# The eight relative-bias tables of a hybrid decoder layer: one product for all of them, and stores that read one partition repeatedly

## The chip, the core and the metric

The kernel runs on one core of a Trainium2 chip, in one launch. The metric is the device time of one execution in microseconds (us), from several runs of the same program on one chip.

## What is computed

The reference is one decoder layer on 1024 tokens of width 1024: a gated feed-forward layer, a mixer with two groups of heads (differential attention and a gated linear recurrence), and a second feed-forward layer, each behind a norm that is shifted and scaled by a conditioning vector. The change touches one input of the attention only, the relative bias:

```python
def t5_bucket(rel):
    n = jnp.maximum(rel, 0)
    ...
    return jnp.where(n < max_exact, n, large)

def diff_attention(q, k, v, rel_bias, lam):
    ...
        s = jnp.einsum('bmqd,bmkd->bmqk', qb, k, preferred_element_type=jnp.float32) * scale
        rel = (start + jnp.arange(Q_BLOCK, dtype=jnp.int32))[:, None] - kpos[None, :]
        bias = jnp.take(rel_bias, t5_bucket(rel), axis=0)
        s = s + jnp.transpose(bias, (2, 0, 1)).astype(jnp.float32)[None]
        s = jnp.where((rel >= 0)[None, None], s, -jnp.inf)
```

There are 32 buckets and 8 maps (4 heads with two each), so `rel_bias` is 32 x 8. A score's bias depends on the distance of query and key alone, and is constant from a distance of 128 on.

## The kernel before

All activations lie transposed or in token rows of 512 columns. Every large product is done in three passes on split fp32 operands (`mm3`, lines 63 to 66): a high part and a remainder, made by one ScalarE cast (line 57) and one VectorE subtraction (line 60). The first feed-forward layer (`f1`) multiplies in blocks: for each of eleven pairs of hidden columns p it runs units of twelve matmuls of 128x512. The last pair is p = 10, its units come in the order 1, 6, 2, 5, 7, 3, 4 with two halves m = 0 and 1 each. A unit of product 1 is followed by a ScalarE copy of its PSUM bank (`f1vp`, line 503), and the unit of product 6 with the same m then adds onto that same bank. The finished hidden parts (`f1vs`, `f1vu` and so on) are stored to DRAM (`f1g`, `f1gt`), combined in place by VectorE (line 391), stored again, and read back (`f1b`) for the second half of the layer, the down products (`f1ps`), which begin at 503.9 us.

The order of the work is not the order of the text. Each piece is recorded as an operation with an engine, an estimated duration, what it reads and writes, and a rank (a due time); `Plan.run` (line 220) then simulates the engines and emits, for each, the operation that can start first, the lower rank first. A tile has a tag with a fixed number of places; the next tile of that tag waits until all use of the last one has ended. The tag `acc` has one place. DMAs all go through SyncE (SP): its queue is in program order, an instruction that has to wait keeps back what stands behind it, and eight DMA semaphores are used in turn, so that a DMA also waits for the eighth before it.

Beside the last units of `f1`, between 450 and 492 us, the kernel builds the bias tables (`bias_table`, lines 991 to 1008). For each map m: VectorE copies the map's column of `rel_bias` to 128 columns (`rbb`, line 996); TensorE multiplies that with a one-hot matrix of buckets (`oh`, line 998), so that all 128 partitions of PSUM hold the same row of 256 biases; VectorE takes off the last bucket's value (lines 1003 and 1004) and appends 128 columns of -1e30 (line 1005); and SP stores the 128 equal rows of 384 elements to a DRAM buffer `wd{m}` (line 1008). The store makes the attention's later load (`near_bias`, line 1356) a plain strided read, one column further left for each query row. The tile `wt{m}` has the tag `acc`, and table m starts after table m - 1.

Then come the scalars of attention and recurrence (`lam_and_rnn_columns`, line 1049): four small loads of the lambda vectors into `lt` (line 1054, tag `acc` too, after the last table's store), a product and a sum on VectorE (lines 1012 and 1013), an exponential on ScalarE (line 1057), and a chain of some two dozen tiny VectorE instructions for a log-sigmoid (lines 1033 to 1047) with an exponential of its own (line 1060).

The names in the profile's rows: `psw` is the bias product, `wt` the table, `wd` the DRAM buffer, `f1w` a split weight, `f1B` a split activation, `kh` and `kl` the split keys of the attention, which SP copies from 64 partitions to the other 64 (line 1352).

Of the kernel before, what the change touches and what calls it, by code (L numbers as in the profile page):

```python
# [10 lines left out]
F32 = mybir.dt.float32  # L11
F32R = mybir.dt.float32r
AF = mybir.ActivationFunctionType
ALU = mybir.AluOpType
# [3 lines left out]
P = 128  # L18
# [7 lines left out]
HEADS = 4  # L26
QK = 64
NBK = 32
EPS = 1e-6
MASK = -1.0e30  # L30
# [14 lines left out]
def layer(tc, I, out):  # L45
    nc = tc.nc
    V, A, G, T = nc.vector, nc.scalar, nc.gpsimd, nc.tensor
    stack = ExitStack()

    def load(o, i):  # L50
        nc.sync.dma_start(out=o, in_=i)
# [27 lines left out]
    def bank(tag, nm):  # L79
        return psp[0].tile([P, TG], F32, tag=tag, bufs=BANKS[tag], name=nm)  # L80
# [47 lines left out]
    wd = [dram.tile([P * 384], F32, name=f"wd{m}") for m in range(2 * HEADS)]  # L128
# [4 lines left out]
    class Plan:  # L133
# [52 lines left out]
        def op(self, eng, fn, dur, r=(), w=(), rank=0.0, lat=None, hold=(), after=(), port=None):  # L186
            durs = dict(zip(eng, dur)) if isinstance(eng, tuple) else {eng: dur}
            deps = {self.last[k] for k in (*r, *w, *after) if k in self.last}
            since = max((self.end.get(k, 0.0) for k in (*r, *w, *after) if k not in self.last), default=0.0)
            for k in w:  # L190
                deps.update(self.reads.get(k, ()))
            n = len(self.ops)
            for k in r:
                self.reads.setdefault(k, []).append(n)
            for k in w:
                self.last[k], self.reads[k] = n, []
            places = sorted({self.place(k) for k in (*r, *w, *hold)} - {None})
            for s in places:
                self.left[s] += 1
            if port is None:  # L200
                tags = {t for k in r if self.place(k) for t in self.tag[self.place(k)]}
                port = not tags & self.PSUM
            self.ops.append((durs, fn, rank, lat, sorted(deps), places, since, tuple(w), port,
                             isinstance(eng, tuple)))
# [120 lines left out]
    PE, ACT, DVE, POOL, SP = "PE", "Act", "DVE", "Pool", "SP"  # L325
# [10 lines left out]
    def new_tile(plan, key, tag, shape=None, dt=F32):  # L336
        def make(t=tag if isinstance(tag, str) else tag[0]):
            if t in BANKS:
                return bank(t, key)
            s = shape or [P, TG]  # L340
            if t in KEPT:
                return KEPT[t].tile(s, dt, tag=t, name=key)
            return phase["fp"].tile(s, dt, tag=t, bufs=FFN_PLACES[t], name=key)

        plan.tile(key, tag, make)
# [412 lines left out]
    plan = Plan(FFN_PLACES, None, 0.2)  # L758
    op, tile, the = plan.op, plan.tile, plan.get
# [141 lines left out]
    def due1(n, k=0):  # L901
        if n < 4 * EARLY:
            return 21.0 + 5.0 * (4 * (n // 6) + k) + T_MM3 * (n % 6)
        return 62.0 + 2.58 * (n - 4 * EARLY)
# [8 lines left out]
    for k in range(KC):  # L913
        at = due1(6 * (k // 4), k % 4) - 5
# [70 lines left out]
    for n, (b, hf) in enumerate(halves):  # L985
        u = 40 + 8 * n
        ada_half(f1, b, hf, due1(u), 2.8, f1.when(u - 2), lambda ps, b=b, hf=hf: ada_columns(b, hf, ps), 1.3,
                 w=[("mod", b, hf)])


    def bias_table(m, at):
        rbb, ps, wt, b31 = (f"{s}{m}" for s in ("rbb", "psw", "wt", "b31_"))
        new_tile(plan, wt, "acc")
        new_tile(plan, rbb, "k2")
        new_tile(plan, ps, ("tr", "av"))
        op(DVE, lambda: V.tensor_copy(the(rbb)[0:NBK, 0:P], the("rb")[0:NBK, m : m + 1].to_broadcast([NBK, P])), 0.2, r=["rb"],
           w=[rbb], rank=at, after=[f"wt{m - 1}"] if m else [("mod", 7, 1)])
        op(PE, lambda: T.matmul(the(ps)[:, 0:256], lhsT=the(rbb)[0:NBK, 0:P], rhs=the("oh")[0:NBK, 0:256], start=True, stop=True), 0.45,
           r=[rbb, "oh"], w=[ps], rank=at)

        def table():
            b = fp.tile([P, 1], F32, tag="b31", bufs=1, name=b31)
            V.tensor_copy(b, the(ps)[:, 0:1])
            V.tensor_scalar(the(wt)[:, 0:256], the(ps)[:, 0:256], b, None, ALU.subtract)
            V.memset(the(wt)[:, 256:384], MASK)

        op(DVE, table, 0.6, r=[ps], w=[wt], rank=at, hold=[rbb])
        op(SP, lambda: load(wd[m].rearrange("(q t) -> q t", t=384), the(wt)[:, 0:384]), 0.3, r=[wt], w=[f"wd{m}"], rank=at)

    def lam_sums():  # L1010
        pr = fp.tile([P, 2, QK], F32, tag="arow", bufs=1, name="lpr")
# [37 lines left out]
    def lam_and_rnn_columns(at):  # L1049
        new_tile(plan, "lt", "acc", [P, 4, QK])  # L1050
        tile("ldt", "z", lambda: small("ldt", 2))
        tile("lw", "z", lambda: small("lw", 16))
        for j, nm in enumerate(("lam_q1", "lam_k1", "lam_q2", "lam_k2")):
            op(SP, lambda j=j, nm=nm: load(the("lt")[:, j, :], I[nm].to_broadcast([P, QK])), 0.3, w=[("lt", j)],
               rank=at - 4, after=["wd7"])
        op(DVE, lam_sums, 0.5, r=[("lt", j) for j in range(4)], w=["ldt"], rank=at)
        op(ACT, lambda: A.activation(the("ldt"), the("ldt"), AF.Exp), 1.5, r=["ldt"], w=["ldt"], rank=at)
        op(DVE, lam_value, 0.2, r=["ldt", "smc"], w=["nlam"], rank=at)
        op(DVE, minus_abs, 0.15, r=["smc"], w=["lw"], rank=at, after=["wd7"])
        op(ACT, lambda: A.activation(the("lw")[:, 4:8], the("lw")[:, 0:4], AF.Exp), 0.2, r=["lw"], w=["lw"], rank=at)  # L1060
        op(DVE, log_sigmoid, 2.0, r=["lw", "smc"], w=["rcol"], rank=at)
# [2 lines left out]
    tile("rb", "z", lambda: small("rb", 8))  # L1064
    op(SP, lambda: load(the("oh")[0:NBK, 0:256], I["onehot"]), 0.1, w=["oh"], rank=due1(126), after=f1.when(126))
    op(SP, lambda: load(the("rb")[0:NBK], I["rel_bias"]), 0.1, w=["rb"], rank=due1(126), after=f1.when(126))
    for m in range(2 * HEADS):
        bias_table(m, due1(128 + 1.5 * m))
    lam_and_rnn_columns(due1(142))


# [72 lines left out]
    for j in range(2):  # L1144
        rc, hi, lo, ps = f"rc{j}", f"wch{j}", f"wcl{j}", f"pc{j}_0"
# [3 lines left out]
           rank=t2 - 10, after=[("f1d4_4", 0)])  # L1149
# [6 lines left out]
        for k in range(KC):  # L1156
# [3 lines left out]
               r=[hi, lo, *x], w=[ps], rank=t2 + j)  # L1160
        op(ACT, lambda j=j, ps=ps: A.activation(the("qf00")[:, j, :], the(ps), AF.Copy, scale=0.125 if j == 0 else 1.0),
           T_CAST, r=[ps], w=[("qf00", j)], rank=t2)
# [29 lines left out]
    for tag in ("tr", "av", "mm"):  # L1192
        bank(tag, tag)
    plan = Plan(
        {"mm": 2, "tr": 1, "z": 8, "av": 1, "d": 2, "p": PB, "qk": 6, "qf": 4, "xr": 2, "v": 4, "at": 2,
         "ln": 3, "nb": 1, "xh": 8, "h": 32, "wh": 4, "raw": 3}, was
    )
    op, tile, the = plan.op, plan.tile, plan.get
# [535 lines left out]
    for j in range(2):  # L1734
        n = next(nch)
        chunk(n)
        f = f"qf0_{j}_0"
# [41 lines left out]
    for dc in range(KC):  # L1779
        n = n0 + dc  # L1780
# [11 lines left out]
    for dc in range(6):  # L1792
        n = n0 + 8 + dc
# [5 lines left out]
    for n, k in enumerate(ORDER):  # L1799
        sq = "n3a" if n == 0 else f"n3s{k}"  # L1800
        if n:
            mkt(sq, "qf", [P, TG], bufs=4)
        op(ACT, lambda sq=sq, k=k: A.activation(the(sq), the(f"x21_{k}"), AF.Square), 0.5, r=[f"x21_{k}"], w=[sq],
           rank=FIRST + 130)
        if n:
            op(DVE, lambda sq=sq: V.tensor_tensor(the("n3a"), the("n3a"), the(sq), ALU.add), 0.62, r=["n3a", sq],
               w=["n3a"], rank=FIRST + 130)
# [24 lines left out]
    plan = f2.plan  # L1832
    op, tile, the = plan.op, plan.tile, plan.get
# [14 lines left out]
    def due2(n):  # L1848
        return t0 + 2.6 * n
# [18 lines left out]
    for k in (0, 4, 1, 5, 2, 6, 3, 7):  # L1868
        x, x2, o = x3[k], f"x21_{k}", 2 * KC + k
        op(DVE, lambda x=x, x2=x2, o=o: V.scalar_tensor_tensor(  # L1870
            the(x), the(x2), gmc[:, o : o + 1], the("n3r"), ALU.mult, ALU.mult), T_DVE, r=["n3r", x2], w=[x],
           rank=t0 - 10)
# [25 lines left out]
    for hf in range(2):  # L1898
# [3 lines left out]
           w=[row], rank=due2(u), after=f2.when(u - 6))  # L1902
        ada_half(f2, 8, hf, due2(u), 5.0, f2.when(u - 6), lambda ps, hf=hf: gate3(hf, ps), 1.2, [row], [row])
        op(SP, lambda hf=hf, row=row: load(g3d[:, hf * TG : (hf + 1) * TG], the(row)[0:1]), 0.1, r=[row],
           w=[f"g3d{hf}"], rank=due2(u + 18))
# [126 lines left out]
def build(shapes):  # L2032
    import concourse.bacc as _bacc
    import concourse.tile as _tile

    nc = _bacc.Bacc("TRN2", target_bir_lowering=False, num_devices=1)
    aps = {n: nc.dram_tensor(f"in_{n}", s, F32, kind="ExternalInput").ap() for n, s in shapes.items()}
    out = nc.dram_tensor("out_0", (1, S, D), F32, kind="ExternalOutput").ap()
    with _tile.TileContext(nc, schedule_with_timeline_sim=True) as tc:
        layer(tc, aps, out)  # L2040
    return nc
# [10 lines left out]
```

## Time and profile before

| | |
|---|---|
| three runs, median (lowest, highest) | 1808.46 us (1805.84, 1812.81) |
| the profiled execution, own time | 1807.46 us |
| its span, first to last instruction | 1805.7 us |
| TensorE (PE) busy | 1769.0 us, 98% of the span |
| VectorE (DVE) busy | 1426.6 us, 79% |
| ScalarE (ACT) busy | 855.2 us, 47% |
| DMA | 297.50 MB, all but 1.5 MB through SP's queue |
| mean granted TensorE clock | 0.992 |

The profile is of one execution. Its times are counted from the first instruction. A row names the line, the engine, the operation and its tiles as out<-in; busy time is the sum of the instructions' durations. Matmuls overlap in the engine's pipeline, so the step from one start to the next tells what a matmul costs, not its duration.

### The profile page before, as it was taken

The page shows a single profiled execution, that of the slowest core. Times are in us where ns is not written, and L with a number is a line of the kernel's source. Part 1 is how long each engine was busy: PE and PEld are TensorE (multiplying, and loading weights), DVE is VectorE, ACT ScalarE, POOL GpSimd, SP SyncE. Part 2 cuts the span into 40 slices and gives each one's busy share as a digit, 9 for nine tenths or more (in the row PEclk, how much of TensorE's full clock was granted, in tenths as well). Part 3 has the DMA queues.
Part 4 walks back from the last instruction along what each step waited for, and adds up shares of the span by engine and source line. Part 5 has one row for each costly group of instructions (what it writes and reads, how often), then busy time and mean ns, then how long its engine had stood idle before and what let it go on. Part 6 is the DMA issues. An engine that isn't in the chain of part 4 may idle for free.

```text
span 1805.7 us, 23739 instructions
## 1 busy us (share of the span) xinstructions
PE 1769.0 (98%) x8182; PEld 1462.4 (81%) x8182; DVE 1426.6 (79%) x2725; ACT 855.2 (47%) x1485; POOL 13.0 (1%) x28
## 2 busy tenths in 40 slices
PE   8999999999999999999999989999999999999997
PEld 7878888888788888788888778878888888888886
DVE  3799998998778779789787786598777666589798
ACT  3543334333454334676675854453333333364344
POOL 0000000000000001000000000000000000000000
PEclk7999999999999999999999999999999999999999
DMA  9635666554597672412112435314434323497862
GB/s 277 203 111 200 204 214 199 187 198 135 195 350 278 222 251 94 105 47 65 53 59 65 129 99 186 120 54 170 155 123 139 127 96 111 152 362 266 284 213 93
DMA packets 230137, 297.50 MB, mean 165 GB/s; under 512 B 16733, under 2 KB 125438, under 8 KB 230018
## 3 DMA queue, kind: packets, MB, share of 16 engines
q1 hardware_dynamic: 230018, 296.00, 49.7%
q8 instruction: 64, 1.05, 0.2%
q14 instruction: 55, 0.45, 0.1%
HBM read 228.30 MB, written 63.44 MB: 162 GB/s over the span
## 4 chain that ended last, share of the span: by engine, by line
PE 87%; DVE 9%; DMA 2%; ACT 1%; issue 1%; SPq 0%; DVEq 0%; ACTq 0%
PE f1b L64 7%; PE f1b L66 7%; PE f1b L65 7%; PE f2b L64 7%; PE f2b L65 7%; PE f2b L66 7%; PE pc L64 5%; PE pc L66 5%; PE pc L65 5%; PE f2ps L64 4%; PE f2ps L65 4%; PE f2ps L66 4%; PE f1ps L66 3%; PE f1ps L65 3%; PE f1ps L64 3%; PE psd L874 2%
## 5 line engine op out<-in xcount | busy, mean ns | idle before, releaser
L64 PE MATMUL f1b<-f1B,f1w 128*128 128x512 f32 x616 | 245.8, 399 | 0.8 <-ACT f1vs L512 0.8
L65 PE MATMUL f1b<-f1B,f1w 128*128 128x512 f32 x616 | 242.7, 394 | 3.6 <-DVE f1w L60 3.6
L66 PE MATMUL f1b<-f1B,f1w 128*128 128x512 f32 x616 | 242.9, 394 | 0.0
L64 PE MATMUL f2b<-f2B,f2w 128*128 128x512 f32 x440 | 171.6, 390 | 1.7 <-ACT f2vq L488 1.4
L65 PE MATMUL f2b<-f2B,f2w 128*128 128x512 f32 x440 | 171.3, 389 | 0.6 <-DVE f2w L60 0.6
L66 PE MATMUL f2b<-f2B,f2w 128*128 128x512 f32 x440 | 171.2, 389 | 0.0
L65 PEld LDWEIGHTS f1b<-f1B,f1w 128*128 128x128 f32 x616 | 116.3, 189 | 29.9 <-DVE f1w L60 4.8
L64 PEld LDWEIGHTS f1b<-f1B,f1w 128*128 128x128 f32 x616 | 116.2, 189 | 29.2 <-issue 2.9
L66 PEld LDWEIGHTS f1b<-f1B,f1w 128*128 128x128 f32 x616 | 116.2, 189 | 26.6
L60 DVE TENSOR_TENSOR f2w<-f2r,f2w 128x512 fp32r<-128x512 f32 x124 | 84.7, 688 | 66.3 <-ACT f2w L57 65.2
L64 PE MATMUL pc<-h,wch 128*128 128x512 f32 x320 | 129.0, 403 | 0.0
L57 ACT ACTIVATE f2w<-f2r 128x512 fp32r<-128x512 f32 x124 | 76.5, 628 | 105.8 <-issue 40.2
L65 PE MATMUL pc<-h,wcl 128*128 128x512 f32 x320 | 125.3, 391 | 0.0
L66 PE MATMUL pc<-h,wch 128*128 128x512 f32 x320 | 125.2, 391 | 0.0
L57 ACT ACTIVATE f1w<-f1r 128x512 fp32r<-128x512 f32 x124 | 76.8, 628 | 96.9 <-PE f1b L66 40.7
L66 PE MATMUL f1ps<-f1o,f1d 128*128 128x512 f32 x308 | 121.2, 394 | 0.0
L64 PE MATMUL f1ps<-f1o,f1d 128*128 128x512 f32 x308 | 121.2, 393 | 0.0
L65 PE MATMUL f1ps<-f1o,f1d 128*128 128x512 f32 x308 | 121.0, 393 | 0.0
L64 PE MATMUL f2ps<-f2d,f2o 128*128 128x512 f32 x308 | 119.9, 389 | 0.1
L66 PE MATMUL f2ps<-f2d,f2o 128*128 128x512 f32 x308 | 119.8, 389 | 0.0
L65 PE MATMUL f2ps<-f2d,f2o 128*128 128x512 f32 x308 | 119.8, 389 | 0.0
L64 PEld LDWEIGHTS f2b<-f2B,f2w 128*128 128x128 f32 x440 | 82.6, 188 | 20.0 <-ACT f2vq L488 1.8
(410 smaller groups left out, 3937.9 us busy)
## 6 DMA issues: line engine op xcount, KB each, us to landing
ar<-in_ada_w SPq DMA_DIRECT2D x112, 256.0 KB, 3.2
f2r<-in_ffn_w SPq DMA_DIRECT2D x44, 512.0 KB, 3.7
f1r<-in_ffn_w SPq DMA_DIRECT2D x40, 512.0 KB, 4.3
f1wa<-in_ffn_w SPq DMA_DIRECT2D x38, 512.0 KB, 5.0
f2wa<-in_ffn_w SPq DMA_DIRECT2D x38, 512.0 KB, 5.8
f1b<-f1gt SPq DMA_DIRECT2D x44, 256.0 KB, 5.8
f2b<-f2gt SPq DMA_DIRECT2D x44, 256.0 KB, 6.0
rc<-in_w_in SPq DMA_DIRECT2D x20, 512.0 KB, 3.7
```

The source lines that it names most:

```text
L57: A.activation(hi, src, AF.Copy)
L60: (eng or V).tensor_tensor(lo, src, hi.bitcast(F32), ALU.subtract)
L64: T.matmul(ps, lhsT=wh, rhs=xl, start=first, stop=False, skip_group_check=more)
L65: T.matmul(ps, lhsT=wl, rhs=xh, start=False, stop=False, skip_group_check=more)
L66: T.matmul(ps, lhsT=wh, rhs=xh, start=False, stop=last, skip_group_check=more)
L874: T.matmul(the(ps)[:, b : b + 1], lhsT=the(aw)[:, n, :], rhs=cact[:, 4 * h + n : 4 * h + n + 1], start=h == 0 and n == 0, stop=h == 1 and ...
```

## The change

One product makes all eight tables: the 32 x 8 matrix `rel_bias` itself is the left operand, so that map m's row of 256 biases lies on partition m alone. One copy, one subtraction and one fill on 8 partitions finish the tables. The eight stores stay, each of 128 rows of 384 elements to the same DRAM buffer, but each now reads its one partition m 128 times (a step of 0 in the source). Nothing that reads `wd` is changed. The tables are one tile `wt`, due at unit 136 in place of 128 to 138.5.

```diff
-    def bias_table(m, at):
-        rbb, ps, wt, b31 = (f"{s}{m}" for s in ("rbb", "psw", "wt", "b31_"))
-        new_tile(plan, wt, "acc")
-        new_tile(plan, rbb, "k2")
-        new_tile(plan, ps, ("tr", "av"))
-        op(DVE, lambda: V.tensor_copy(the(rbb)[0:NBK, 0:P], the("rb")[0:NBK, m : m + 1].to_broadcast([NBK, P])), 0.2, r=["rb"],
-           w=[rbb], rank=at, after=[f"wt{m - 1}"] if m else [("mod", 7, 1)])
-        op(PE, lambda: T.matmul(the(ps)[:, 0:256], lhsT=the(rbb)[0:NBK, 0:P], rhs=the("oh")[0:NBK, 0:256], start=True, stop=True), 0.45,
-           r=[rbb, "oh"], w=[ps], rank=at)
+    def bias_tables(at):
+        n = 2 * HEADS
+        new_tile(plan, "wt", "acc")
+        new_tile(plan, "psw", ("tr", "av"))
+        op(PE, lambda: T.matmul(the("psw")[0:n, 0:256], lhsT=the("rb")[0:NBK, 0:n], rhs=the("oh")[0:NBK, 0:256],
+                                start=True, stop=True), 0.45, r=["rb", "oh"], w=["psw"], rank=at, after=[("mod", 7, 1)])
 
         def table():
-            b = fp.tile([P, 1], F32, tag="b31", bufs=1, name=b31)
-            V.tensor_copy(b, the(ps)[:, 0:1])
-            V.tensor_scalar(the(wt)[:, 0:256], the(ps)[:, 0:256], b, None, ALU.subtract)
-            V.memset(the(wt)[:, 256:384], MASK)
-
-        op(DVE, table, 0.6, r=[ps], w=[wt], rank=at, hold=[rbb])
-        op(SP, lambda: load(wd[m].rearrange("(q t) -> q t", t=384), the(wt)[:, 0:384]), 0.3, r=[wt], w=[f"wd{m}"], rank=at)
+            b = fp.tile([P, 1], F32, tag="b31", bufs=1, name="b31")
+            V.tensor_copy(b[0:n], the("psw")[0:n, 0:1])
+            V.tensor_scalar(the("wt")[0:n, 0:256], the("psw")[0:n, 0:256], b[0:n], None, ALU.subtract)
+            V.memset(the("wt")[0:n, 256:384], MASK)
+
+        op(DVE, table, 0.6, r=["psw"], w=["wt"], rank=at)
+        for m in range(n):
+            op(SP, lambda m=m: load(wd[m].rearrange("(o q t) -> o q t", o=1, t=384),
+                                    the("wt")[m : m + 1, 0:384].unsqueeze(1).to_broadcast([1, P, 384])), 0.3, r=["wt"],
+               w=[f"wd{m}"], rank=at)
...
-    for m in range(2 * HEADS):
-        bias_table(m, due1(128 + 1.5 * m))
+    bias_tables(due1(136))
```

The planner emits another order from there on. On SP before, the first stores of tables stand between the stores of hidden parts (each row with what it waits for; `DMAHW` are the eight semaphores of the DMAs, used in turn):

```order
L51 DMA f1g_9_166<-f1vv_0_4004 128x512 [waits DMAHW3_49,DVE_49]
L51 DMA wd_119<-wt_4119 128x384 [waits DMAHW4_49,DVE_49]
L51 DMA f1g_9_144<-f1vs_4086 128x512 [waits DMAHW5_49,DVE_49]
L51 DMA wd_120<-wt_4147 128x384 [waits DMAHW6_49,DVE_49]
L51 DMA f1gt_9_188<-f1vs_4086 128x512 [waits DMAHW7_49,DVE_49]
```

and the lambda loads follow twenty-four rows after the first of these stores:

```order
L51 DMA lt<-in_lam_q 128x64 [waits DMAHW4_49,DMAHW5_49,DMAHW1_49,DMAHW0_49]
L51 DMA lt<-in_lam_k 128x64
L51 DMA lt<-in_lam_q 128x64
L51 DMA lt<-in_lam_k 128x64 [waits DMAHW7_49]
L51 DMA f1b_3_4464<-f1g_3_160 128x512 [waits DVE_49]
```

With the change, SP's queue at the same place (after six stores like the first two here):

```order
L51 DMA wd_125<-wt 128x1x384 [waits DMAHW2_49]
L51 DMA wd_126<-wt 128x1x384 [waits DMAHW3_49]
L51 DMA f1g_9_144<-f1vs_4086 128x512 [waits DMAHW4_49,DVE_49]
L51 DMA lt<-in_lam_q 128x64 [waits DMAHW5_49,DMAHW3_49,DMAHW6_49,DMAHW2_49,DMAHW7_49,DMAHW1_49,DMAHW0_49]
L51 DMA lt<-in_lam_k 128x64
L51 DMA lt<-in_lam_q 128x64
L51 DMA lt<-in_lam_k 128x64
L51 DMA f1g_9_177<-f1vu_0_3910 128x512 [waits DVE_49]
L51 DMA f1gt_9_188<-f1vs_4086 128x512 [waits DVE_49]
```

The eight stores now stand in a row, the store of the hidden part `f1vs` of p = 9 has moved behind them, and the lambda loads, which need the place of `wt`, stand right after it and wait for the stores.

On VectorE with the change, beside the last units of p = 9 and the first of p = 10 (`f1vu`, `f1vs`, `f1vp`: hidden parts of p = 9; `lw`: the log-sigmoid):

```order
L518 TENSOR_TENSOR f1vu_1_3947<-f1vu_1_3947,f1b_9_1_4041 128x512
L522 TENSOR_TENSOR f1vu_0_3910<-f1vu_0_3910,f1vu_1_3947 128x512
L391 TENSOR_TENSOR f1vs_4086<-f1vp_0_3866,f1vs_4086 128x512
L1034 TENSOR_SCALAR lw<-lw 128x4
L1035 RECIPROCAL lw<-lw 128x4
```

and, twenty-two tiny instructions on `lw` further (new line numbers are one above the old):

```order
L1046 TENSOR_SCALAR rcol<-lw 128x4
L1047 TENSOR_SCALAR rcol<-lw 128x4
L1048 TENSOR_SCALAR rcol<-smc 128x8
L1013 TENSOR_TENSOR lpr<-lt 128x128
L1014 TENSOR_REDUCE ldt<-lpr 128x2
L391 TENSOR_TENSOR f1vp_0_3866<-f1vu_0_3910,f1vp_0_3866 128x512
L60 TENSOR_TENSOR f1w_4176<-f1s_0_3976,f1w_4176 128x512
```

Before, VectorE had all of p = 9 and nearly all weights of p = 10 behind it when it came to `lw` and `lt`; now these two stand ahead of the last work of p = 9 and of the weights from product 5 on.

On ScalarE before, at the first units of p = 10:

```order
L503 ACTIVATE f1vp_0_4209<-f1b_10_0_4175 128x512
L57 ACTIVATE f1w_4220<-f1s_1_4027 128x512
L57 ACTIVATE f1o_0_0_4223<-f1b_0_4045 128x512
L57 ACTIVATE f1o_0_0_4232<-f1b_0_4053 128x512
L503 ACTIVATE f1vp_1_4247<-f1b_10_1_4204 128x512
```

and with the change:

```order
L503 ACTIVATE f1vp_0_4224<-f1b_10_0_4169 128x512
L57 ACTIVATE f1w_4229<-f1s_1_4027 128x512
L57 ACTIVATE f1o_0_0_4231<-f1b_0_4045 128x512
L1058 ACTIVATE ldt<-ldt 128x2
L503 ACTIVATE f1vp_1_4256<-f1b_10_1_4220 128x512
```

The exponential of the lambdas has moved ahead of the copy of the bank onto which product 6 with m = 1 adds. On PE nothing changes but that seven of the eight bias products are gone.

## Rows read from the trace of the kernel before

**Rows 1.** The page: the span, each engine's busy time, the chain that ended last.

```profile
span 1805.7 us, 23739 instructions
...
PE 1769.0 (98%) x8182; PEld 1462.4 (81%) x8182; DVE 1426.6 (79%) x2725; ACT 855.2 (47%) x1485; POOL 13.0 (1%) x28
...
PE 87%; DVE 9%; DMA 2%; ACT 1%; issue 1%; SPq 0%; DVEq 0%; ACTq 0%
```

**Rows 2.** Busy time in stretches: us and instructions by engine, PE's clock, DMA share, GB/s.

```profile
450.00:480.00 30.00, 30.00 (x120) 20.95 (x119) 21.19 (x53) 10.63 (x19) 0.00 (x0) 1.00 0.55 187
25.00:30.00 5.00, 5.00 (x24) 4.90 (x24) 1.32 (x4) 1.00 (x2) 0.00 (x0) 0.50 1.12 286
30.00:40.00 10.00, 10.00 (x46) 8.68 (x44) 1.87 (x4) 2.16 (x6) 0.00 (x0) 0.66 1.08 302
```

**Rows 3.** The chain of waits from 449 to 453 us: start, us, engine and line.

```profile
450.00 0.24 PE f1b L66
450.24 0.62 PE psw L998 x2
450.86 0.43 PE f1b L64
451.30 0.24 PE f1b L65
```

**Rows 4.** The tables' instructions: count, shortest/median/longest in ns, first and last start.

```profile
L996 DVE COPY rbb<-rb x8: 150/151/207, 449.8 to 476.9; 32x128 f32<-32x128 f32 x8
...
L1003 DVE COPY b<-psw x8: 149/151/157, 450.9 to 480.3; 128x1 f32<-128x1 f32 x8
L1004 DVE TENSOR_SCALAR wt<-psw,b x8: 483/484/485, 451.1 to 480.4; 128x256 f32<-128x256 f32 x8
...
L1005 DVE MEMSET wt<- x8: 165/165/165, 451.6 to 480.9; 128x128 f32 x8
L51 SPq DMA_DIRECT2D wd<-wt x8: 319/319/338, 451.7 to 481.1; - x8
```

**Rows 5.** SP's queue in time order: a table's store, the lambda loads, a copy of keys.

```profile
451.75 0.32 SPq L51 DMA_DIRECT2D wd<-wt  x1
452.51 0.32 SPq L51 DMA_DIRECT2D f1g<-f1vs  x1
...
483.34 0.33 SPq L51 DMA_DIRECT2D lt<-in_lam_q  x1
...
484.67 0.43 SPq L51 DMA_DIRECT2D lt<-in_lam_k  x1
...
739.02 0.46 SPq L51 DMA_DIRECT2D kl<-kl  x1
```

**Rows 6.** Busy time in two short stretches, columns as in rows 2.

```profile
452.80:453.00 0.20, 0.20 (x2) 0.00 (x0) 0.20 (x1) 0.00 (x0) 0.00 (x0) 1.00 0.99 369
739.70:740.00 0.30, 0.30 (x3) 0.24 (x2) 0.27 (x2) 0.27 (x2) 0.00 (x0) 1.00 0.91 198
```

**Rows 7.** The page's DMA issues: count, KB each, median us to landing.

```profile
f1g<-f1vs SPq DMA_DIRECT2D x11, 256.0 KB, 2.2
...
kl<-kl SPq DMA_DIRECT2D x16, 128.0 KB, 2.9
...
wd<-wt SPq DMA_DIRECT2D x8, 192.0 KB, 1.8
```

**Rows 8.** DVE in time order.

```profile
458.99 0.69 DVE L518 TENSOR_TENSOR f1vu<-f1vu,f1b 128x512 f32<-128x512 f32 x1 [0.15 <-PE f1b L66]
...
485.07 0.17 DVE L1033 TENSOR_SCALAR lw<-lw 128x4 f32<-128x4 f32 x1 [0.77 <-ACT lw L1060]
...
489.72 0.16 DVE L1047 TENSOR_SCALAR rcol<-smc 128x8 f32<-128x8 f32 x1
...
490.40 0.29 DVE L1012 TENSOR_TENSOR lpr<-lt 128x128 f32<-128x128 f32 x1
490.73 0.29 DVE L1013 TENSOR_REDUCE ldt<-lpr 128x2 f32<-128x128 f32 x1
...
503.82 0.69 DVE L391 TENSOR_TENSOR f1vs<-f1vp,f1vs 128x512 f32<-128x512 f32 x1 [2.20 <-DMA f1g<-f1vs]
```

**Rows 9.** ACT in time order: product 1's bank copied (m = 1); the lambdas' exponential.

```profile
466.16 0.60 ACT L503 ACTIVATE f1vp<-f1b 128x512 f32<-128x512 f32 x1 [1.40 <-PE f1b L66]
...
491.05 0.20 ACT L1057 ACTIVATE ldt<-ldt 128x2 f32<-128x2 f32 x1 [2.43 <-DVE ldt L1013]
```

**Rows 10.** PE in time order: a bias product, then product 6 with m = 1.

```profile
468.78 0.69 PE L998 MATMUL psw<-oh,rbb 32*128 32x256 f32 x2
469.41 0.50 PE L64 MATMUL f1b<-f1B,f1w 128*128 128x512 f32 x1
```

## The prediction

> **What bounds the kernel now.** I read the page first: PE is busy for 98% of the span and makes 87% of the chain that ended last [rows 1], so time is won where PE does less and lost where PE has to wait. Then the stretch of the change: from 450 to 480 us PE has no gap at all, while DVE is busy for 21.2 of 30 us and the DMA engines for 55% [rows 2]. The chain of waits there runs along PE alone, through the bias products [rows 3]. So DVE's and SP's part in the tables is hidden now, and the eight products are not.
>
> **What goes.** A bias product and the matmul behind it take 0.62 and 0.43 us of the chain, where the matmul alone takes 0.24 [rows 3]: one product costs 0.81 us. Seven go: -5.7 us on the path. On DVE each table goes with 0.15 + 0.15 + 0.48 + 0.17 us [rows 4]; seven make 6.7 us, all of it beside a busy PE [rows 2], worth nothing by itself. The remaining product, copy, subtraction and fill have the same number of columns on fewer partitions; I take their times as they are. ACT's two table loads only move; ACT is busy for a third of the stretch [rows 2].
>
> **What the new stores cost.** This is the term that decides. A store still moves 128 x 1536 B = 196.6 kB, but out of one partition, eight times in a row. No row shows a large transfer out of so few partitions, so I bound it.
> - Low end: as fast as now. The first store is issued at 451.75 us [rows 5]; while its packets run the engines are 99% busy and move 369 GB/s [rows 6]. That is 0.53 us a store, 4.3 us for eight.
> - High end: a partition gives no more than one DMA engine draws now, 369/16 = 23.1 GB/s, since the engines share the 128 rows out and each works through its own. That is 8.5 us a store, 68 us for eight.
> - The nearest row: a copy of keys reads 64 partitions and writes the other 64 (it is issued at 739.02 us [rows 5]). While it runs, the same sixteen engines at 91% move 198 GB/s, 218 at full share, against 369/0.99 = 373 for the table [rows 6]. All engines are at work in both, so what halves the rate is the number of partitions, not of engines. 218 GB/s over eight groups of eight partitions is 27.2 GB/s a group; a store out of one partition meets one group: 7.2 us, eight 57.8 us.
>
> I take 58 us, because only that row has fewer than 128 partitions under full load. It cannot tell reading from writing, which is the weak point. A share by single partitions (218/64 = 3.4 GB/s, 462 us for eight) I leave out: an engine draws 23.1 GB/s now while it works on its rows.
>
> [...]
>
> **Who waits for them.** The rows of the changed order say so, and here everything moved counts.
> 1. SP's queue: the eight stores are issued from 451.75 us on, 0.32 us each [rows 4, 5]; their data begin near 452.6 and, at 57.8 us, end at 510.4.
> 2. The store of `f1vs`, which stood between two tables [rows 5], is behind them. It waits for the first store's semaphore and its packets then queue on the same engines. 256 KB are 0.7 us at 373 GB/s and some 0.5 us more to landing (a table lands 1.8 us after issue [rows 7], of which 0.85 pass before its data and 0.5 in them): 511.5 us.
> 3. DVE comes to the in-place L391 on `f1vs` at about 459: it follows the `f1vu` work of 458.99 [rows 8], 1.6 us earlier by the two products gone ahead of it. It cannot overwrite the tile before that store has landed; the same wait shows elsewhere as 2.2 us [rows 8]. DVE stops until 511.5.
> 4. Behind it stand L391 itself (0.69), the log-sigmoid chain (485.07 to 489.88, 4.8 us) and the two lambda sums (490.40 to 491.02, 0.6) [rows 8]. The four lambda loads wait for the last table at 510.9, take 1.7 us to issue [rows 5] and some 2 to land, 514.6: before DVE needs them at 517.0. They are not last.
> 5. ACT's exponential of the lambdas now stands ahead of the copy of product 1's bank, m = 1. It adds 0.2 us, the copy 0.6 [rows 9], and the handover to PE some 0.2.
> 6. PE can go on with product 6, m = 1, at 511.5 + 0.7 + 4.8 + 0.6 + 0.2 + 0.6 + 0.3 = 518.7. It would be there at 469.41 [rows 10] less five products, 465.4. PE waits 53.3 us, that is 4.5 less than the stores take.
>
> What else is queued on SP (the other stores of p = 9, the first blocks of the down products) starts some 50 us late with PE, and nothing else uses the engines then; I count no further stall.
>
> **TensorE's clock.** PE idles for 50 us, which it never does before. [...] I take 2.
>
> **Sum,** from the profiled execution's 1807.46 us (1.0 below the median of the three runs): 1807.46 - 5.7 + 53.3 + 2 = **1857 us**, 2.7% slower.
>
> **Rivals.**
> - *Repeated reading costs nothing* (only writing is bound by partitions). The stores then end near 457, DVE meets no wait, does L391 until 459.6, the chain until 464.4, the sums until 465.0, and PE goes on at 466.1 in place of 465.4: 0.8 us given back. 1807.46 - 5.7 + 0.8 = 1802.6 us, 0.3% faster, within what a measurement of this kernel can tell from no change (0.5%, 9 us). For it: the key copy reads and writes half the partitions at once, and its limit may lie with the writes. Against: nothing in the rows makes reading the freer side. It decides wherever the eight stores take less than about 10 us, where the wait equals the 5.7 us saved; up to 19 us the loss stays within 0.5%.
> [...]
> - *Sixteen engines that take turns at one partition get less than one engine alone*: at half the rate, 116 us and 1915 us. No row shows such a loss; in the key copy the group's 27.2 GB/s is above an engine's 23.1.
> - *The stores don't spread over the engines*, since the source has one row only: one engine at 23.1 GB/s needs 68 us for eight, other DMAs pass it, and the lambda loads become the last wait, 452.6 + 68 + 0.5 + 1.7 + 2 = 524.8, PE on at 526.4: 1865 us. That is the forecast's own price by another way, and I count it there.
>
> **How the numbers follow.** The forecast with the one-engine form 0.70, its own range 1850 (55 us, no loss by the clock) to 1872 (70 us, 3.4); free reading 0.13; two groups 0.10; turns 0.07. From 1822 to 1885 the range holds the first and the third, 0.80. The median of the runs before lies at 1808.46: slower by over 0.5% are all but free reading, 0.87; of that I give 0.11 to no change and 0.02 to faster, should PE lose nothing back and a gain follow from the lighter DVE.
>
> **What would show it.** Right: `psw` once on PE; eight `wd` stores issued within some 4 us near 452, the last to land near 511; in that stretch few GB/s (27) at a DMA share near full; one PE gap of 45 to 65 us from about 465, put down to ACT's `f1vp`, and behind it a DVE wait of some 50 us for the store of `f1vs`; afterwards the same stages as before, moved. Wrong: `wd` landing within a few us of issue, no PE gap, a span near 1801; or a gap with another end, such as weights or the lambda loads.

## The result and the profile after

| | before | after |
|---|---|---|
| median of four runs each, on one chip | 1807.82 us | 1859.18 us |
| ratio, 95% interval | | 1.0284, 1.0269 to 1.0298 |
| the profiled execution, own time | 1807.46 us | 1856.02 us |

The change makes the kernel 2.8% slower; predicted were 1857.0 us. The page of the changed kernel has the same head as [rows 1]: the span, the busy times, the chain that ended last.

```profile
span 1854.2 us, 23664 instructions
...
PE 1767.2 (95%) x8168; PEld 1464.1 (79%) x8168; DVE 1422.3 (77%) x2696; ACT 856.0 (46%) x1485; POOL 13.6 (1%) x28
...
PE 85%; DVE 8%; DMA 3%; SPq 2%; ACT 1%; issue 1%; ACTq 0%; DVEq 0%
```

PE does less (1767.2 us for 1769.0) in a longer span. In the chain PE falls from 87 to 85% and SP's queue (SPq) has 2% where it had 0; these shares alone don't name the place. The windows, columns as in [rows 2], do:

```profile
450.00:480.00 30.00, 15.72 (x68) 11.91 (x66) 7.27 (x15) 5.57 (x9) 0.00 (x0) 0.83 0.77 25
480.00:500.00 20.00, 0.00 (x0) 0.00 (x0) 0.00 (x0) 0.00 (x0) 0.00 (x0) 0.50 0.87 30
500.00:520.00 20.00, 2.73 (x7) 2.16 (x8) 8.62 (x39) 2.73 (x6) 0.00 (x0) 0.50 0.55 88
```

From 480 to 500 us no engine computes, the DMA engines are busy for 87% and move 30 GB/s; before, at 55%, they moved 187 GB/s in 450 to 480 us [rows 2]. The waits of 440 to 560 us (who for whom: sum, times, longest) name the links:

```profile
ACT ldt L1058 <- DVE ldt L1014: 54.6, 1, 54.6
...
DVE f1vs L391 <- DMA f1g<-f1vs: 51.8, 2, 51.6
PE f1b L64 <- ACT f1vp L503: 51.5, 1, 51.5
```

The rows of each engine in time order, SP first:

```profile
451.89 41.14 SPq L51 DMA_DIRECT2D wd<-wt  x8
493.13 7.12 SPq L51 DMA_DIRECT2D f1g<-f1vs  x1
510.09 0.34 SPq L51 DMA_DIRECT2D lt<-in_lam_q  x1
```

DVE:

```profile
458.28 0.69 DVE L522 TENSOR_TENSOR f1vu<-f1vu,f1vu 128x512 f32<-128x512 f32 x1
510.56 0.69 DVE L391 TENSOR_TENSOR f1vs<-f1vp,f1vs 128x512 f32<-128x512 f32 x1 [51.59 <-DMA f1g<-f1vs]
511.17 0.16 DVE L1034 TENSOR_SCALAR lw<-lw 128x4 f32<-128x4 f32 x1
...
515.88 0.28 DVE L1013 TENSOR_TENSOR lpr<-lt 128x128 f32<-128x128 f32 x1
516.20 0.29 DVE L1014 TENSOR_REDUCE ldt<-lpr 128x2 f32<-128x128 f32 x1
```

ACT:

```profile
516.52 0.20 ACT L1058 ACTIVATE ldt<-ldt 128x2 f32<-128x2 f32 x1 [54.59 <-DVE ldt L1014]
516.63 0.58 ACT L503 ACTIVATE f1vp<-f1b 128x512 f32<-128x512 f32 x1
```

PE, which stopped behind a matmul of 465.33:

```profile
465.33 0.39 PE L66 MATMUL f1b<-f1B,f1w 128*128 128x512 f32 x1
517.27 0.80 PE L64 MATMUL f1b<-f1B,f1w 128*128 128x512 f32 x1 [51.55 <-ACT f1vp L503]
517.86 0.63 PE L65 MATMUL f1b<-f1B,f1w 128*128 128x512 f32 x1
```

So the chain is: stores, store of `f1vs`, DVE's in-place sum, the log-sigmoid and the lambda sums, ACT's exponential, ACT's copy of `f1vp`, PE. Three short windows hold PE's return, with its clock third from the end:

```profile
517.30:518.50 1.20, 1.20 (x3) 1.01 (x4) 1.17 (x5) 1.20 (x3) 0.00 (x0) 0.50 0.46 176
518.50:521.00 2.50, 2.50 (x7) 1.92 (x7) 2.50 (x7) 0.76 (x2) 0.00 (x0) 0.50 0.85 288
521.00:522.00 1.00, 1.00 (x6) 0.81 (x5) 1.00 (x3) 0.00 (x0) 0.00 (x0) 0.91 0.93 291
```

PE comes back at a granted clock of 0.50 until about 521.2: 3.7 x 0.5 + 0.1 = 1.9 us lost. The balance of the two profiled executions: -5.7 (seven products) + 51.5 + 1.9 = +47.7 us, against 1856.02 - 1807.46 = +48.6.

The stores' rows (shortest, median, longest issue; first and last start), beside [rows 4]:

```profile
L51 SPq DMA_DIRECT2D wd<-wt x8: 580/6810/7185, 451.9 to 485.8; - x8
L1002 DVE TENSOR_SCALAR wt<-psw,b x1: 472/472/472, 451.2 to 451.2; 8x256 f32<-8x256 f32 x1
...
DMA to landing us min/median/max: 24.1/24.7/24.7
```

A store lands 24.7 us after its issue began, where it took 1.8 [rows 7], and the issue itself takes 6.8 us. By the trace's packet records, the 1024 packets of 1536 B run from 453.1 to 509.5 us: 1.573 MB in 56.4 us, 27.9 GB/s, one packet 780 ns (before: 65).

### The profile page after: what moved, and what is told of

Read it like the earlier page. It is cut to its first block, busy times and chain, and to the rows that moved or that the text cites. A ratio compares the mean times of both kernels' runs of the same rounds, so it can differ in the third digit from the quotient of the medians.

```text
span 1854.2 us, 23664 instructions
## 1 busy us (share of the span) xinstructions
PE 1767.2 (95%) x8168; PEld 1464.1 (79%) x8168; DVE 1422.3 (77%) x2696; ACT 856.0 (46%) x1485; POOL 13.6 (1%) x28
## 4 chain that ended last, share of the span: by engine, by line
PE 85%; DVE 8%; DMA 3%; SPq 2%; ACT 1%; issue 1%; ACTq 0%; DVEq 0%
PE f1b L64 7%; PE f1b L66 7%; PE f1b L65 7%; PE f2b L64 6%; PE f2b L65 6%; PE f2b L66 6%; PE pc L64 5%; PE pc L65 5%; PE pc L66 5%; PE f1ps L66 4%; PE f1ps L64 4%; PE f1ps L65 4%; PE f2ps L64 3%; PE f2ps L66 3%; PE f2ps L65 3%; SPq L51 2%
## 5 line engine op out<-in xcount | busy, mean ns | idle before, releaser
L64 PE MATMUL f1b<-f1B,f1w 128*128 128x512 f32 x616 | 246.1, 399 | 52.8 <-ACT f1vp L503 51.5
```

Source lines behind the costliest of these rows:

```text
L64: T.matmul(ps, lhsT=wh, rhs=xl, start=first, stop=False, skip_group_check=more)
```

## The experiments

Two questions are open with the result: what about the source is slow (that it repeats, or where it lies), and what carries the stores' time to PE (the order of SP's queue, or the DMA engines).

### Fewer partitions, one at a time

The kernel before, with the source of the stores alone changed:

```diff
-        op(SP, lambda: load(wd[m].rearrange("(q t) -> q t", t=384), the(wt)[:, 0:384]), 0.3, r=[wt], w=[f"wd{m}"], rank=at)
+        n = (64, 32, 16, 8, 4, 2, 1, 1)[m]
+        op(SP, lambda: load(wd[m].rearrange("(q r t) -> q r t", q=n, t=384),
+                            the(wt)[0:n, 0:384].unsqueeze(1).to_broadcast([n, P // n, 384])), 0.3, r=[wt], w=[f"wd{m}"], rank=at)
```

> The kernel before, with its order and its eight products; only the source of the stores is narrowed: table 0's store reads 64 partitions, each twice, table 1's 32, then 16, 8, 4, 2, 1 and 1. The output is the same. It measures the reading price by itself. Theory G (a group of partitions has one rate, 27 GB/s for eight of them as worked out from the key copy): 64 partitions 0.9 us, 32 1.8, 16 3.6, and 8, 4, 2, 1 all alike, 7.1 us. Theory P (each single partition has its own rate, 27.9 GB/s as the changed kernel shows for one, and sixteen are enough to keep the engines full): 0.53 us for 64, 32 and 16, then 0.9, 1.8, 3.5, 7.1, 7.1. Theory R (the repeating step in the source is what is slow, wherever it lies): all eight about 7 us. [...] The time: the tables still come 4 us apart, so under G or P the last few stores back up by 3 us each, 10 to 15 us in all, near the end of the first layer; 1808 to 1818 us, under R 1808 + about 30.

Measured: 1838.67 us (one run) beside a median of 1808.07. The packet records of each store (1536 B each, 128 a store); "engines at work" is the sum of their times over the stretch:

| partitions read | first to last packet, us | median packet, ns | engines at work | other data meanwhile, kB |
|---|---|---|---|---|
| 64 | 1.6 | 114 | 11.3 | 120 |
| 32 | 1.3 | 113 | 11.5 | 81 |
| 16 | 2.7 | 218 | 11.1 | 176 |
| 8 | 4.7 | 216 | 6.3 | 327 |
| 4 | 7.7 | 220 | 3.1 | 950 |
| 2 | 7.8 | 109 | 1.8 | 467 |
| 1 | 7.2 | 773 | 12.7 | 0 |
| 1 | 7.3 | 778 | 12.7 | 151 |

The windows of the stores from 4, 2 and 1 partitions show the same in DMA share and GB/s (the last two numbers, all traffic):

```profile
476.00:483.00 7.00, 3.50 (x13) 2.44 (x11) 0.00 (x0) 2.15 (x4) 0.00 (x0) 0.89 0.57 151
486.00:493.00 7.00, 5.99 (x15) 4.35 (x15) 0.51 (x2) 0.63 (x1) 0.00 (x0) 0.63 0.37 91
496.00:502.80 6.80, 6.80 (x20) 5.39 (x20) 0.76 (x2) 1.73 (x4) 0.00 (x0) 0.61 0.83 28
```

Theory R falls: with two and four repeats a store takes 1.6 and 1.3 us, not 7. Theory P falls: 16 partitions (2.7 us) are not as fast as 64 (1.6), and 1 (7.2 us) is no slower than 2 (7.8). That fewer DMA engines are at work from 8 partitions on is not the reason either: at the 65 ns a packet of the kernel before, 3.1 engines would pass 128 packets in some 3 us, an estimate, where 7.7 were measured. What remains is G, with groups that differ from mine: 32 neighbours are as fast as 64 (1.3 and 1.6 us), so partitions 32 to 63 added no group here, and 4, 2 and 1 are alike (7.7, 7.8 and 7.2 us), so four neighbours act as one. Groups of four at the 7.2 us of one partition would give 3.6, 1.8 and 0.9 us for 8, 16 and 32 partitions, an estimate; measured are 0.4 to 1.1 us more, and the other data of the last column may be why, which isn't shown.

The time misses the 1808 to 1818 us expected. The tile of the tables has one place, so DVE waits for each store before the next table, and PE for its operand:

```profile
DVE wt L1004 <- DMA wd<-wt: 27.1, 7, 9.1
...
PE psw L998 <- DVE rbb L996: 10.9, 3, 5.2
```

PE's row in the last window has its clock at 0.61 after these stops. Its gaps come to 16.6 us between 470 and 540 us, and its clock stands at 0.50 for 23.9 us there, some 12 us more: 28 of the 31 us lost. I had left both out.

### One product, sixteen partitions a table

From the changed kernel: the columns of `rel_bias` are copied 16 times, one product still makes all tables, and a store reads 16 partitions eight times each. In the spread form table m lies on every eighth partition from m, in the block form on 16m to 16m + 15.

```diff
+        op(DVE, lambda: V.tensor_copy(the("rbb")[0:NBK, 0:P].rearrange("k (c m) -> k c m", m=n), the("rb")[0:NBK, 0:n].unsqueeze(1).to_broadcast([NBK, P // n, n])), 0.2, r=["rb"], w=["rbb"],
...
-            op(SP, lambda m=m: load(wd[m].rearrange("(o q t) -> o q t", o=1, t=384),
-                                    the("wt")[m : m + 1, 0:384].unsqueeze(1).to_broadcast([1, P, 384])), 0.3, r=["wt"],
-               w=[f"wd{m}"], rank=at)
+            op(SP, lambda m=m: load(wd[m].rearrange("(q r t) -> q r t", q=16, t=384),
+                                    the("wt")[m : P : n, 0:384].unsqueeze(1).to_broadcast([P // n, n, 384])), 0.3, r=["wt"], w=[f"wd{m}"], rank=at)
```

> The changed kernel, with the same order of stores and loads, but the product's left operand holds the eight columns sixteen times in turn (one more VectorE copy), so table m lies on the partitions m, m + 8, m + 16 and so on, and each store reads these sixteen, each eight times. Theory G or P (the place of the source is what is slow): the sixteen lie in all groups, a store takes 0.5 to 0.9 us, eight at most 7.2 us, done by 460 when VectorE comes to the f1vs work; no gap on PE to speak of; 5.7 us saved, 0.8 given back to the longer VectorE order: 1802 to 1804 us, ratio 0.997 to the kernel before. Theory R (repeating is slow): stores of 7 us again, PE gap of some 51 us, ratio 1.028. That the order alone, without slow stores, makes the wait: a gap of PE in spite of short stores; more than 3 us of it would say so.

> As the spread form, but table m's sixteen copies lie next to each other, on partitions 16m to 16m + 15, each read eight times. Theory P: sixteen partitions are enough, 0.53 us a store, ratio 0.997 as in the spread form. Theory G with groups of eight: two groups, 3.5 us a store, eight 28 us, ended at 481; by the prediction's steps VectorE goes on at 482 and PE at 489 in place of 465.4, 23.6 us: 1807.5 - 5.7 + 23.6 + 1 = 1826 us, ratio 1.010. Theory R: as the changed kernel, 1.028. [...]

Measured: spread 1807.51 us, ratio 0.9993 (0.9978 to 1.0007); block 1810.80 us, 1.0009 (0.9998 to 1.0020). By the packets the eight stores take 7.8 us spread, 10.1 us in blocks, for 56.4. Spread, the waits of DVE, PE and the clock behind them:

```profile
461.22 0.69 DVE L391 TENSOR_TENSOR f1vs<-f1vp,f1vs 128x512 f32<-128x512 f32 x1 [3.03 <-DMA f1g<-f1vs]
...
467.95 0.50 PE L64 MATMUL f1b<-f1B,f1w 128*128 128x512 f32 x1 [3.01 <-ACT f1vp L503]
...
468.00:470.00 2.00, 2.00 (x8) 1.65 (x9) 1.97 (x7) 1.94 (x4) 0.00 (x0) 0.87 0.56 194
...
470.00:474.00 4.00, 4.00 (x13) 3.15 (x12) 3.56 (x6) 1.12 (x2) 0.00 (x0) 0.64 0.90 267
```

Same chain, 3.0 us instead of 51.5. The gap is followed by 2 us at 0.87 and 4 at 0.64, 2 x 0.13 + 4 x 0.36 = 1.7 us more: -5.7 + 3.0 + 1.7 = -1.0 us; 0.9993 is -1.3, between -4.0 and +1.3. The block form has a gap of 5.4 us:

```profile
472.86 0.80 PE L64 MATMUL f1b<-f1B,f1w 128*128 128x512 f32 x1 [5.42 <-ACT f1vp L503]
```

So short stores are not enough; my 0.8 us given back left out that the store of `f1vs` still stands behind them. The block form's 10.1 us are less than eight stores would take one after the other: sixteen neighbours, as four groups of four at the 27.9 GB/s of one partition, give 1.8 us a store and 14 us in all, an estimate from the first experiment and the changed kernel's stores. So stores of different blocks might overlap. The next run tests that alone.

### One partition a table, the tables 16 apart

The block form, each store reading the first of its sixteen partitions 128 times (the lines of the source, against the changed kernel):

```diff
-                                    the("wt")[m : m + 1, 0:384].unsqueeze(1).to_broadcast([1, P, 384])), 0.3, r=["wt"],
+                                    the("wt")[16 * m : 16 * m + 1, 0:384].unsqueeze(1).to_broadcast([1, P, 384])), 0.3, r=["wt"], w=[f"wd{m}"], rank=at)
```

> As the block form, but each store reads a single partition, 16m, 128 times: the store of the changed kernel with the eight sources 16 partitions apart. If the stores go through one after the other, as the queue has them, each still meets one group: 7.1 us a store, PE gap of some 51 us, ratio 1.028 as the changed kernel. [...]

Measured: 1835.97 us, ratio 1.0157 (1.0139 to 1.0174); the stores take 34.0 us, and the gap of PE is

```profile
494.70 0.79 PE L64 MATMUL f1b<-f1B,f1w 128*128 128x512 f32 x1 [29.23 <-ACT f1vp L503]
```

The eight go neither one after the other (56.4 us in the changed kernel) nor all at once, but nearly two side by side: 1.573 MB in 34.0 us, 46 GB/s for 27.9. Why two is not shown. So stores from different places do overlap, but the change's own layout hardly reaches that: by the first experiment's times its first four tables, on four neighbours, share one group (7.7 us from 4 partitions, 7.2 from 1), and the next four add another (4.7 us from 8). In the packet records of the changed kernel only one us stands out, about where the fifth store follows the fourth: 49 packets began from 481 to 482, at a median of 65 ns, for 15 to 23 in each other us from 453 to 508.

### The order of SP's queue

One dependency more in the changed kernel: the stores are issued after the first store of `f1vs`.

```diff
-               w=[f"wd{m}"], rank=at)
+               w=[f"wd{m}"], rank=at, after=["f1g11_9"])
```

> The changed kernel with its slow stores and that one dependency: the first store of f1vs is issued ahead of the eight. Theory (whoever is next behind the stores becomes the wait): PE runs through product 6 and product 2, m = 0 and 1, and product 5, m = 0, to about 477; then VectorE stands at the second in-place sum of f1vs, whose second store comes behind the eight (landing at about 511), and behind that stand another sum 0.7, the lambda sums (loads landed about 514.6) 0.6, and the weight for product 5, m = 1, 0.7: PE on at 516.4, gap 39 us, 1807.5 - 5.7 + 39.3 + 1.8 = 1843 us, ratio 1.0196. If instead the wait for f1vs were the only one, the gap would vanish: ratio 0.998. If the clogged engines and not the order were the cause, the first store of f1vs would not be helped and the gap stay near 51 us: 1.028.

And, in another kernel, the stores stay ahead of `f1vs`, but the lambda loads and the log-sigmoid no longer wait for them:

```diff
-        new_tile(plan, "lt", "acc", [P, 4, QK])
+        new_tile(plan, "lt", "k2", [P, 4, QK])
...
-               rank=at - 4, after=["wd7"])
+               rank=at - 4, after=[("mod", 7, 1)])
...
-        op(DVE, minus_abs, 0.15, r=["smc"], w=["lw"], rank=at, after=["wd7"])
+        op(DVE, minus_abs, 0.15, r=["smc"], w=["lw"], rank=at, after=[("mod", 7, 1)])
```

> The changed kernel; only the four lambda loads get another place in memory (tag k2) and no longer wait for the tables: they stand ahead of the eight stores, and the log-sigmoid chain and the lambda sums run on VectorE before the wait. The store of f1vs stays behind the eight. Theory: VectorE still waits at the first in-place sum of f1vs until 511.2, but the weights of product 2 now stand ahead of it, so PE runs to about 474 and waits there for the weight of product 5, m = 0: 511.2 + 0.7 + 0.5 + 0.7 + 0.7 + 0.4 = 514.2, gap 40 us; 1807.5 - 5.7 + 40 + 1.8 = 1843.6 us, ratio 1.020. If the lambda loads were the cause (the last link), the gap goes and the ratio is 0.998; if their place did nothing, 51 us and 1.028.

Measured: 1845.65 us, ratio 1.0195 (1.0170 to 1.0220), and 1850.31 us, 1.0224 (1.0202 to 1.0247). With `f1vs` ahead, DVE and PE:

```profile
513.79 0.69 DVE L391 TENSOR_TENSOR f1vs<-f1vu,f1vs 128x512 f32<-128x512 f32 x1 [43.94 <-DMA f1gt<-f1vs]
518.83 0.29 DVE L1013 TENSOR_TENSOR lpr<-lt 128x128 f32<-128x128 f32 x1 [3.62 <-DMA lt<-in_lam_k]
...
520.73 0.80 PE L64 MATMUL f1b<-f1B,f1w 128*128 128x512 f32 x1 [41.94 <-ACT f1vu L503]
```

With the lambda loads ahead:

```profile
508.25 0.69 DVE L391 TENSOR_TENSOR f1vs<-f1vp,f1vs 128x512 f32<-128x512 f32 x1 [48.98 <-DMA f1g<-f1vs]
...
510.51 0.80 PE L65 MATMUL f1b<-f1B,f1w 128*128 128x512 f32 x1 [38.73 <-DVE f1w L60]
```

As expected, whoever stands next behind the stores becomes the wait, and only the three or four units that PE can still do in between are won. In the first the gap is 41.9 us for 39.3: its last link was not the weight, but the lambda loads, which came 3.6 us late, and ACT's copy of a bank behind the exponential, as in the change. In the second the gap is 38.7 for 40, yet the time is above the expected 1.020; PE has another 3.1 us of small gaps between 520 and 560 us and runs partly at half clock (0.50 from 510 to 515 us, 0.80 from 545 to 550).

### The stores in another queue

The last kernel again, its stores issued by POOL:

```diff
-            op(SP, lambda m=m: load(wd[m].rearrange("(o q t) -> o q t", o=1, t=384),
-                                    the("wt")[m : m + 1, 0:384].unsqueeze(1).to_broadcast([1, P, 384])), 0.3, r=["wt"],
-               w=[f"wd{m}"], rank=at)
+            op(POOL, lambda m=m: G.dma_start(out=wd[m].rearrange("(o q t) -> o q t", o=1, t=384),
+                                    in_=the("wt")[m : m + 1, 0:384].unsqueeze(1).to_broadcast([1, P, 384])), 0.3, r=["wt"],
+               w=[f"wd{m}"], rank=at, lat=2.5)
```

> As the run before this one (lambda loads ahead), but the eight slow stores are issued by POOL, in a queue of its own, so that nothing of SP's stands behind them. It parts SP's order from the clogged engines. If only the order of the queue counts, and the sixteen engines serve SP's packets while the others wait for their partition: no gap, ratio 0.997. If an engine takes the two queues in turn, packet by packet, SP gets one of 2048 B (84 ns) for each slow one (780 ns): 16 x 2048 B / 864 ns = 38 GB/s for 57 us, where this stretch wants 187; PE starves for weights, gaps of up to 45 us in all, ratio 1.015 to 1.022. If the engines are simply blocked until the eight are through: as the run before, 1.020 or more.

Measured: 1847.81 us, ratio 1.0206 (1.0184 to 1.0228), beside 1.0224 (1.0202 to 1.0247) with SP's queue, so no difference clear of noise. SP's queue, which now holds none of the stores:

```profile
451.85 0.33 SPq L51 DMA_DIRECT2D f1g<-f1vs  x1
460.75 0.33 SPq L51 DMA_DIRECT2D f1g<-f1vu  x1
469.45 7.34 SPq L51 DMA_DIRECT2D f1gt<-f1vs  x1
476.89 12.91 SPq L51 DMA_DIRECT2D f1gt<-f1vp  x1
489.89 18.51 SPq L51 DMA_DIRECT2D f1wb<-in_ffn_w  x2
```

and DVE and PE:

```profile
468.73 0.69 DVE L391 TENSOR_TENSOR f1vs<-f1vp,f1vs 128x512 f32<-128x512 f32 x1 [8.01 <-DMA f1g<-f1vs]
...
510.38 0.69 DVE L391 TENSOR_TENSOR f1vs<-f1vu,f1vs 128x512 f32<-128x512 f32 x1 [37.63 <-DMA f1gt<-f1vs]
...
512.46 0.80 PE L65 MATMUL f1b<-f1B,f1w 128*128 128x512 f32 x1 [30.17 <-DVE f1w L60]
```

and the view of DMA issues (count, KB, us to landing):

```profile
f1g<-f1vu SPq DMA_DIRECT2D x1, 256.0 KB, 49.0
```

PE's gaps between 450 and 560 us come to 38.0 us, for 41.8 in the run before. A transfer that meets no store in its own queue takes 17 us (451.85 to 468.7) instead of 2.2 [rows 7], the next one 49: it was issued at 460.75, but by the packet records none of its data start before 497.0. From 461 to 495 us the engines are 95% busy and move 30 GB/s in all:

```profile
461.00:495.00 34.00, 18.13 (x79) 14.25 (x77) 3.98 (x9) 3.45 (x7) 0.00 (x0) 0.87 0.95 30
```

So the slow stores hold up SP's queue too, though none of them stands in it. Packets in turn would have given SP 38 GB/s all along; it got 37 from 460 to 464 us, and no data packet started from 467.1 to 497.0. In these runs the order of the queue decides who is caught, but another queue does not escape. That SP's packets are held in the DMA engines, and not in what prepares them, is the likely reading of the 95% and isn't shown by itself.

### Two forms that keep the gain

The spread form with the dependency above:

> The spread form (sixteen interleaved copies, a store in 0.96 us) with one more dependency: the eight stores are issued after the first store of f1vs of p = 9, so that this one stands ahead of them in SP's queue as it did before the change. In the spread form PE had one gap of 3.0 us, put down to the same chain as the change's 51.5 us, and behind it 3.7 us at half clock, 1.7 us lost: 5.7 - 3.0 - 1.7 = 1.0 us saved, where 1.3 were measured. Theory (the order of SP's queue makes the wait, the stores' length sizes it): with the store of f1vs ahead there is no gap, the clock stays at 1.00 there, and the whole 5.7 us are saved: 1802.4 us, ratio 0.9968. Rival (another wait takes its place, the second in-place sum of f1vs on its second store, which stays behind the eight): a gap of about 3 us again, ratio 0.999. If the 5.7 us are not there to be had at all (weights for p = 10 are late): no gap at 465, but smaller ones after it, ratio 0.999.

And one partition a table, with the repeating done in DRAM: the eight rows are stored once (12 KB), and the stores read them there.

```diff
+        op(SP, lambda: load(td.rearrange("(m t) -> m t", t=384), the("wt")[0:n, 0:384]), 0.3, r=["wt"], w=["td"], rank=at,
+           after=["f1g11_9"])
         for m in range(n):
             op(SP, lambda m=m: load(wd[m].rearrange("(o q t) -> o q t", o=1, t=384),
-                                    the("wt")[m : m + 1, 0:384].unsqueeze(1).to_broadcast([1, P, 384])), 0.3, r=["wt"],
-               w=[f"wd{m}"], rank=at)
+                                    td[m * 384 : m * 384 + 384].rearrange("(o p t) -> o p t", o=1, p=1).to_broadcast([1, P, 384])), 0.3,
+               r=["td"], w=[f"wd{m}"], rank=at)
```

> The changed kernel with one partition a table, but the eight rows go to DRAM once (12 KB), and the eight stores read their row there 128 times instead of from SBUF; the whole is issued after the first store of f1vs, as in the ordered spread form. It asks whether the repeating source is dear by itself or the SBUF partition is. If the SBUF partition is what is slow: reading one DRAM row 128 times is bounded by the engines, 0.53 to 1 us a store, eight within 10 us, behind some 2 us for the small store; no gap of PE at 465, ratio 0.997 as the ordered spread form. If a row that is read over and over is slow wherever it lies: 7 us a store again, the wait of the second store of f1vs, ratio 1.019. Between them, a DRAM row at half the engines' rate or so would still end by 472 and cost nothing.

Measured: 1803.44 us beside 1807.77, ratio 0.9970 (0.9956 to 0.9985); and 1802.65 us beside 1808.37, ratio 0.9966 (0.9952 to 0.9979). The window of the spread form with the order:

```profile
450.00:480.00 30.00, 30.00 (x130) 24.02 (x129) 23.77 (x74) 13.52 (x24) 0.00 (x0) 1.00 0.50 148
```

and of the DRAM form, with its stores:

```profile
450.00:480.00 30.00, 30.00 (x131) 23.96 (x130) 22.53 (x71) 14.30 (x25) 0.00 (x0) 1.00 0.55 184
...
L51 SPq DMA_DIRECT2D wd<-td x8: 588/596/600, 458.7 to 463.2; - x8
```

No gap, full clock: 5.4 us saved (2.7 to 8.0) and 6.1 (3.8 to 8.7), where seven products were put at 5.7. In the DRAM form a store still reads one row 128 times and a packet takes 65 ns, as in the kernel before (780 in the changed kernel, from one SBUF partition): the repeating costs the packets nothing, the SBUF partition did. With the same dependency and the row read from SBUF the ratio was 1.0195.

## Why the prediction was right

The time came out at 1859.18 us for 1857.0 forecast, and the profile has the steps in the order that the prediction gave them.

- **Seven products, -5.7 us.** `psw` is on PE once. The two last forms bring -5.4 and -6.1.
- **The stores, 57.8 us.** 56.4 measured, 27.9 GB/s for 27.2. The number was right and its ground half so. The rate of the key copy was measured [rows 6], its division into eight groups of eight partitions was my assumption, and the first experiment speaks for another: four neighbours act as one group (7.7 us from 4 partitions, 7.2 from 1), and 64 are no faster than 32 (1.6 and 1.3 us), which again makes eight groups of 64 partitions. That the count came out at eight all the same was luck. The copy in the window of [rows 6] is that of `kh`, issued at 738.22 us (the packets of `kl` begin at 740.1); it has the same shape, so the rate stands.
- **Step 1.** The eight issues were to be over in some 4 us. SP is held 41.1 us by them. It cost nothing more, as everything behind them in the queue had to wait for the data in any case.
- **Steps 2 and 3.** The store of `f1vs` was to land at 511.5; DVE goes on at 510.56, after a wait of 51.6 us, for the reason given.
- **Step 4.** L391, the chain and the sums were put at 0.7 + 4.8 + 0.6 = 6.1 us; DVE takes from 510.56 to 516.49, 5.9. The lambda loads were in time: L1013 starts without a wait.
- **Steps 5 and 6.** PE goes on at 517.27 instead of 518.7, as the stores take 1.4 us less. The gap is 51.5 us for 53.3.
- **The clock, 2 us.** 1.9 measured, for 3.7 us at 0.50 and 1 us at 0.91 behind the wait. No run before showed what the clock does behind a wait: the 2 was a choice between nothing and 3.4 us, the loss of 10 us at the 0.66 in [rows 2], so the closeness is luck.
- **The rivals.** Free reading, turns at less than an engine's rate, and the one-engine form are out by the 27.9 GB/s and the 13.4 engines at work (the sum of the packets' times over 56.4 us). Two groups of four tables with their stores side by side (0.10 of the chances) would have taken half of the 56.4 us, and are out here; stores overlapped with the tables 16 partitions apart (34.0 us).
- **The sum,** -5.7 + 53.3 + 2 = +49.6 us, measured +48.6 between the profiled executions (the rows sum to +47.7).

What the prediction did not have is the second cause. It let the packets of the store of `f1vs` queue on the same DMA engines (step 2), but put the wait down to the order of SP's queue, and had nothing on transfers of another queue. For this order the two cannot be told apart; with the slow stores neither of the two other orders nor POOL's queue mended it (1.0195 to 1.0224). Stores put off until nothing waits behind them were not tried.

## What to carry to other kernels

Here a store's time followed from where its SBUF rows lie, and not from its bytes: the same 196.6 kB took 1.3 us from 32 partitions and 7 to 8 us from four neighbours or fewer (25 to 28 GB/s). While the eight one-partition stores ran, little else moved, in their queue or in another (0.2 and 0.8 MB in 56 us). Where one row must be repeated, spread copies over the partitions with the product that makes them, or repeat from DRAM; with the store that others wait for issued first, both kept the whole gain (5.4 and 6.1 us, where 5.7 were put). Work saved on the bound engine is soon lost by one wait of its length, and a little more by the half clock behind it: here 5.7 us were saved, 51.5 us waited and 1.9 us more lost at 0.50.

## What was not expected of the hardware

- **The issue blocks.** Of the eight stores the first two issues take 0.6 us each (0.32 with 128 plain rows), the third 4.5, and the last five 6.4 to 7.2 us, about as long as a store's data takes. SP does nothing else meanwhile; issues of other tiles are held 7 and 13 us, too, while the slow stores run in POOL's queue.
- **How many engines a small source occupied followed its shape.** From 4 and 2 partitions, written as 4 x 32 and 2 x 64 rows, 3.1 and 1.8 engines were at work, and other data moved beside them (151 and 91 GB/s in all); from 1 partition, 1 x 128 rows, it was 12.7, and 28 GB/s in all, though the store took hardly less time (7.2 us for 7.7 and 7.8). Whether the change's wait would shrink with its stores in a shape for few engines wasn't tried.
- **POOL's queue joins rows.** There the packets are of 4608 B and 3072 B, not 1536, and one of 4608 B takes 2.58 us: the same 28 GB/s.
- **The half clock followed a gap of only 3.0 us.** In the spread form it came 1.5 us after PE had gone on: 0.87 from 468 to 470 us and 0.64 from 470 to 474 in the rows above.
